# Where the values of an attention unit stand in the DMA queue of a hybrid decoder block

## The chip, the cores and the metric

The kernel runs on one core of a Trainium2 chip. The metric is the device time of one execution in microseconds (us); shorter is better. The core has TensorE (PE, matrix products), VectorE (DVE), ScalarE (ACT), GpSimd (POOL) and SyncE (SP); SP issues all the data transfers (DMAs) of this kernel, in one queue and in a fixed order, and 16 DMA engines carry them out. Each engine works through its own list of instructions in order and waits, where it has to, for a semaphore that another engine or a DMA raises. TensorE writes to PSUM, the other tiles lie in SBUF, and DRAM tiles hold what is put aside.

## The reference

A decoder block for x of 1024 positions by 1024 channels, in float32: a normalisation, one wide projection, two attention branches side by side, gates, an output projection and a normalisation again. Cut to the two branches:

```python
qa, ka, va, fa, za, qb, kb, vb, zb, gates = jnp.split(rms_norm(x, g_pre) @ w_in, ...)
# branch a: 8 heads of 64, with a forget gate; c = cumsum(log_sigmoid(fa + b_forget))
p = softmax(causal(qa @ ka.T / 8 + c[t] - c[s]));    ya = (p @ va) * silu(za)
# branch b: 4 heads of two query/key pairs of 64 (rotated by rope), values of 128
p = softmax(causal(q1 @ k1.T / 8)) - lam * softmax(causal(q2 @ k2.T / 8))
yb = rms_norm(p @ vb, g_subln) * (1 - lam_init) * silu(zb)
merged = sigmoid(gate_a) * (ya @ w_branch[0]) + sigmoid(gate_b) * (yb @ w_branch[1])
out = x + rms_norm(merged @ w_out, g_post)
```

## The kernel before, in words

Products are made in two parts: each float32 operand is split into a rounded high part and the rest (`hi`, `lo`), and three products (hi by hi, hi by lo, lo by hi) are summed in PSUM.

**Stage 1** (lines 119 to 222) normalises and transposes x into `hT`, projects the values of all heads (`v_block`, tiles `pv`) and puts them aside in DRAM as `vb_d` (branch b) and `va_d` (branch a), split into both parts. It ends at about 110 us of the span.

**Stage 2** (lines 251 to 647) is the attention. It has eight units: units 0 to 3 are the four heads of branch b ("diff", tile names that end in d), units 4 to 7 two heads each of branch a ("fox", names in f). For a unit u:

- `unit_proj` (line 271) projects keys and queries, in two chunks of 512 positions each, with weights loaded and split by `load_w` (line 225: `raw_k`, `raw_q`, `hi_k`, `lo_k` and so on). For diff units `rope` (line 280) copies the PSUM tile to `rawk` or `rawq` (line 283), swaps its quarters by four DMAs into `swk` or `swq` (line 287), multiplies `raw` by the cosines on VectorE (line 288) and `sw` by the sines on GpSimd (line 289), and adds them (line 290). `stack` (line 293) then writes the high and low parts into `TA`, `TB` (queries) and `KA`, `KB` (keys).
- `swapped` (line 401) makes the exchanged queries `X0` and `X1` of a group of 256 positions: two DMAs each (line 407), which swap the upper and lower halves of `TA` or `TB`. There are three buffers of each, so they can be made ahead.
- `s_row` (line 410) computes the scores of 128 positions in PSUM (lines 421 and 422; the second takes X), VectorE takes them over with the mask and their row minimum (line 423), ScalarE takes the exponential (line 428), VectorE the reciprocal (line 430).
- `av` (line 433) transposes the probabilities (line 450), splits them (lines 453, 454) and multiplies them by the values `V` (line 474); `evac` writes the result to DRAM (`y_d`, lines 523 and 555).
- `unit_attn` (line 485) allocates the value tile `V` of the unit (line 489: 128 partitions by 8 by 256 values, two buffers) and gives back `load` and the list of `groups`. `load` issues the DMA of `V` (line 495) and, for fox units, two broadcasts `cb` (line 500).

The loop over units (lines 618 to 645) calls `unit_attn(u, T)` and `load()` first. Then it goes through the groups: 4 in a diff unit, 8 in a fox unit (4 per head). It traces the rows of a group, then the `av` of the group before it (`pend`), then a share of `fill`: the projections of the next unit, those of the gate paths `z` (tiles `pz`), and small work. So the last `av` of unit u comes behind the first rows of unit u+1.

**What sets the order.** The tracing order is not the order of execution. When the program is built, a planner with a timeline of its own (`schedule_with_timeline_sim=True`, line 1011) places each instruction on its engine's list as soon as its inputs are there and its buffer is free by that timeline; what was traced earlier goes first among those that are ready. `V` has two buffers, so both unit 0's and unit 1's are free from the start, and V of unit u has to wait for the last product of unit u-2.

**Stages 3 and 4** (lines 654 to 972) compute the gates, the branch products and the output projection. The change does not touch them.

Of the kernel before, what the change touches and what calls it, by code (L numbers as in the profile page):

```python
# [41 lines left out]
def f32(ap):  # L42
    return ap.bitcast(F32)
# [3 lines left out]
def tile_hybrid_block(  # L47
# [18 lines left out]
    nc = tc.nc  # L66
# [184 lines left out]
    with ExitStack() as st:  # L251
# [75 lines left out]
        def z_tasks(t):  # L327
            return spill_tasks(f"z{t}", (ZA + t * P) if t < 4 else (ZB + (t - 4) * P), z_d[t])
# [72 lines left out]
        def swapped(T, m, g, nm):  # L401

            src = T["TB" if m else "TA"]
            qs = slice(2 * g * P, (2 * g + 2) * P)
            t = qk.tile([P, 2 * P], F32R, tag=f"X{m}", name=f"X{m}{nm}_{g}", bufs=3)
            for a, b in ((UPR, DNR), (DNR, UPR)):
                nc.sync.dma_start(f32(t[a]), f32(src[b, qs]))
            return t

        def s_row(T, m, i, X, bias, boff, nm):  # L410

            A, B = (T["TA"], T["KA"]) if m == 0 else (T["TB"], T["KB"])
            n = (i + 1) * P
            qs = slice(i * P, (i + 1) * P)
            xs = slice(i % 2 * P, (i % 2 + 1) * P)
            pr = pp.tile([P, S], F32, tag="P", name=f"P{nm}_{m}_{i}")
            mx = small.tile([P, 2], F32, tag="mx", name=f"mx{nm}_{m}_{i}", bufs=8)
            pcs = pieces(i)
            for j, (a, b) in enumerate(pcs):
                ps = sps.tile([P, CH], F32, tag="S", name=f"S{nm}_{m}_{i}_{j}")[:, 0:b - a]  # L420
                nc.tensor.matmul(ps, lhsT=A[:, qs], rhs=B[:, a:b], start=True, stop=False)  # L421
                nc.tensor.matmul(ps, lhsT=X[:, xs], rhs=B[:, a:b], start=False, stop=True)
                nc.vector.tensor_tensor_reduce(  # L423
                    out=pr[:, a:b], in0=ps, in1=bias[:, boff + a:boff + b], scale=-0.125,
                    scalar=BIG if j == 0 else mx[:, j - 1:j], op0=ALU.add, op1=ALU.min,
                    accum_out=mx[:, j:j + 1])
            le = small.tile([P, 1], F32, tag="l", name=f"l{nm}_{m}_{i}", bufs=8)
            nc.scalar.activation(pr[:, 0:n], pr[:, 0:n], AF.Exp,  # L428
                                 bias=mx[:, len(pcs) - 1:len(pcs)], scale=-1.0, accum_out=le)
            nc.vector.reciprocal(le, le)  # L430
            return pr, le
# [53 lines left out]
        def unit_attn(u, T):  # L485

            diff = u < 4
            t = u if diff else u - 4
            vt = qk.tile([P, NB, 256], F32R, tag="V", name=f"V{u}")
            src = (vb_d if diff else va_d)[:, t, :].rearrange("(b p) c -> p b c", p=P)  # L490
            cb = []
            groups = []

            def load():
                nc.sync.dma_start(f32(vt), src)
                if not diff:
                    for m in range(2):
                        b = big.tile([P, S], F32, tag="big", name=f"cb{u}_{m}")
                        h = 2 * t + m
                        nc.sync.dma_start(b, cum_d[h:h + 1, :].to_broadcast([P, S]))  # L500
                        cb.append(b)

            if diff:
                def row(i, rows):
                    boff = S - (i + 1) * P
                    if "X" not in rows:
                        rows["X"] = [swapped(T, m, i // 2, f"d{u}") for m in range(2)]
                    p1, l1 = s_row(T, 0, i, rows["X"][0], dmask, boff, f"d{u}")
                    p2, l2 = s_row(T, 1, i, rows["X"][1], dmask, boff, f"d{u}")
                    n = (i + 1) * P  # L510
                    nc.vector.tensor_tensor(l2, l2, nlam, op=ALU.mult)  # L511
                    nc.gpsimd.tensor_scalar(  # L512
                        p2[:, 0:n], p2[:, 0:n], l2, 1.0, op0=ALU.mult, op1=ALU.mult)
                    nc.scalar.activation(p1[:, 0:n], p1[:, 0:n], AF.Copy, scale=l1)
                    nc.gpsimd.tensor_tensor(
                        p1[:, 0:n], p1[:, 0:n], p2[:, 0:n], op=ALU.add)
                    rows[i] = p1

                def evac(g):
                    def run(yp):  # L520
                        ys = stg.tile([P, 2 * P], F32, tag="ys", name=f"ys{u}_{g}")
                        nc.scalar.copy(ys, yp)
                        nc.sync.dma_start(y_d[u][:, g * 2 * P:(g + 1) * 2 * P], ys)
                    return run

                for g in GORD[u]:
                    rows = {}
                    groups.append((
                        4 * g + 3,
                        [lambda i=i, rows=rows: row(i, rows) for i in (2 * g, 2 * g + 1)],  # L530
                        lambda g=g, rows=rows: av(rows, g, vt, 0, False, evac(g), f"d{u}_{g}", False)))
            else:
                ysb = {}

                def row(m, i, rows):
                    n = (i + 1) * P
                    diag = cb[m][:, n - P:n]
                    nc.gpsimd.tensor_tensor(diag, diag, trim, op=ALU.add)  # L538
                    if "X" not in rows:
                        rows["X"] = swapped(T, m, i // 2, f"f{u}")  # L540
                    p1, l1 = s_row(T, m, i, rows["X"], cb[m], 0, f"f{u}")
                    nc.gpsimd.tensor_scalar(  # L542
                        p1[:, 0:n], p1[:, 0:n], l1, 1.0, op0=ALU.mult, op1=ALU.mult)
                    rows[i] = p1

                def evac(m, g):
                    def run(yp):
                        if m == 0:
                            ysb[g] = stg.tile([P, 2 * P], F32, tag="ys", name=f"ys{u}_{g}")
                        tmp = stg.tile([P, 2 * P], F32, tag="yt", name=f"yt{u}_{m}_{g}", bufs=1)  # L550
                        nc.scalar.copy(tmp[64:128], yp[64:128])
                        nc.vector.tensor_tensor(
                            ysb[g][64 * m:64 * m + 64], yp[0:64], tmp[64:128], op=ALU.add)
                        if m == 1:
                            nc.sync.dma_start(y_d[u][:, g * 2 * P:(g + 1) * 2 * P], ysb[g])
                    return run

                for g in GORD[u]:
                    for m in range(2):
                        rows = {}  # L560
                        groups.append((
                            4 * g + 3,
                            [lambda m=m, i=i, rows=rows: row(m, i, rows) for i in (2 * g + 1, 2 * g)],
                            lambda m=m, g=g, rows=rows: av(
                                rows, g, vt, m * P, True, evac(m, g), f"f{u}_{m}_{g}",
                                u == 7 and g in FING)))
            return load, groups


        lt = pp.tile([P, 4, 64], F32, tag="P", name="lt")  # L570
# [43 lines left out]
        T, tasks = unit_proj(0)  # L614
        for tk in tasks:
            tk()
        pend = None
        for u in range(8):
            load, groups = unit_attn(u, T)
            if u == 1:  # L620
                forget_sums()
            load()
            fill = []
            if u + 1 < 8:
                T, tasks = unit_proj(u + 1)
                fill += tasks
            for t in ZFILL[u]:
                fill += z_tasks(t)
            fill[2:2] = [lambda k=k: h_combinations(k) for k in TFILL[u]]
            for t in SFILL[u]:  # L630
                fill += [lambda t=t, c=c: sum_squares(t, c) for c in range(2)]
                fill.append(lambda t=t: subln_scales(t))
            total = sum(s[0] for s in groups)
            done, nf = 0, 0
            for n, (wgt, rws, prd) in enumerate(groups):
                for r in rws:
                    r()
                if pend:
                    pend()
                pend = prd  # L640
                done += wgt
                while nf < len(fill) and nf < len(fill) * done / total:
                    fill[nf]()
                    nf += 1
# [370 lines left out]
```

## Time and profile before

| what | value |
|---|---|
| median of 3 runs | 958.73 us |
| lowest, highest | 956.02, 959.63 us |
| the profiled execution's own time | 960.13 us |
| its span, first to last instruction | 958.0 us |
| its mean granted TensorE clock | 0.982 |

How to read the lines quoted below. Times are microseconds, unless a mean is marked ns. L495 is line 495 of the kernel. A tile's buffer number and unit are left out of its name: `V<-vb_d` is a load of any diff unit's values, `X0d<-TA` an exchange. In a line in order of time the first number is the start, counted from the start of the span, the second the duration, x2 the number of instructions merged into the line; brackets hold the idle time before it and what ended that. SPq is SP's queue: its durations are those of the issue, not of the transfer. In a view by stretches the columns are the stretch, its length, busy time of PE, PEld (weight loads, which overlap with PE), DVE, ACT and POOL, each with its count, then the granted TensorE clock as a share of full speed, the mean busy share of the 16 DMA engines, and GB/s.

### The profile page before, as it was taken

The numbers are of one execution on the slowest core, as the hardware profiler recorded it, in microseconds if no ns is written. First come the engines' busy times: TensorE is split into PE (matmuls) and PEld (weight loads), VectorE is DVE, ScalarE is ACT, GpSimd is POOL, SyncE is SP. The second block draws the span as 40 slices with busy tenths as digits, with TensorE's granted clock in tenths as the row PEclk, the third lists the DMA queues.
The fourth block names the chain that finished last, engine by engine and source line by source line (L and its number), as shares of the span: only waits on it lengthen the run. The fifth ranks groups of instructions, "written<-read, shape, count | busy, mean of one in ns | idle before, by whom it ended". The sixth has DMA issues, their size and how long they took to land.

```text
span 958.0 us, 13760 instructions
## 1 busy us (share of the span) xinstructions
PE 900.7 (94%) x4600; PEld 752.1 (79%) x4600; DVE 627.2 (65%) x1180; ACT 437.0 (46%) x862; POOL 489.6 (51%) x460
## 2 busy tenths in 40 slices
PE   7999989899999999999999988999999999999992
PEld 5999867787887888888878877777888768887871
DVE  7731258978768868578676478228665782559875
ACT  3521125665656574565745658323443550324331
POOL 7200035446545466464644575216655735878972
PEclk9999999999999999999999999998999989999997
DMA  9532454434334353534434350893445696210144
GB/s 314 193 110 91 142 134 114 105 80 123 97 94 138 95 155 116 154 122 130 143 123 136 103 186 28 325 377 122 139 138 172 186 370 203 73 38 1 48 150 154
DMA packets 115656, 136.95 MB, mean 143 GB/s; under 512 B 10609, under 2 KB 80241, under 8 KB 114562
## 3 DMA queue, kind: packets, MB, share of 16 engines
q1 hardware_dynamic: 115586, 136.08, 44.4%
q8 instruction: 36, 0.59, 0.3%
q14 instruction: 34, 0.28, 0.1%
HBM read 85.65 MB, written 37.81 MB: 129 GB/s over the span
## 4 chain that ended last, share of the span: by engine, by line
PE 58%; DVE 13%; POOL 8%; DMA 7%; issue 6%; ACT 5%; SPq 2%; DVEq 0%; POOLq 0%; ACTq 0%
PE x_g L713 11%; PE pv L195 9%; PE pb L848 9%; PE pz L246 7%; PE pk L246 4%; PE pq L246 3%; PE ypf L474 3%; PE pg L246 2%; PE ptf L450 2%; DMA swk<-rawk 2%; SPq L287 1%; DVE Pd L423 1%; PE ypd L474 1%; PE Sf L421 1%; DVE wo_op L890 1%
## 5 line engine op out<-in xcount | busy, mean ns | idle before, releaser
L195 PE MATMUL pv<-wvhi,hT 128*128 128x264 f32 (+2 forms) x384 | 89.3, 325 | 0.4 <-DVE hT L181 0.4
L246 PE MATMUL pk<-hT,hi_k 128*128 128x512 f32 x256 | 83.9, 401 | 4.2 <-DVE KB L298 2.4
L246 PE MATMUL pz<-hT,hi_z 128*128 128x512 f32 x256 | 85.1, 400 | 0.0
L848 PE MATMUL pb<-yT,hi_br 128*128 128x512 f32 x256 | 80.8, 398 | 1.9 <-ACT hi_br L232 1.6
L246 PE MATMUL pq<-hT,hi_q 128*128 128x512 f32 x256 | 82.3, 395 | 0.0
L713 PE MATMUL x_g<-T,a_g 128*128 128x512 f32 x336 | 79.5, 392 | 1.6 <-ACT a_g L664 1.2
L713 PE MATMUL x_o<-wo_op,a_o 128*128 128x512 f32 x336 | 77.4, 391 | 2.4 <-ACT a_o L664 1.2
L713 PEld LDWEIGHTS x_o<-wo_op,a_o 128*128 128x128 f32 x336 | 62.8, 188 | 16.9 <-ACT a_o L664 2.1
L713 PEld LDWEIGHTS x_g<-T,a_g 128*128 128x128 f32 x336 | 63.5, 190 | 15.7 <-ACT a_g L664 1.6
L195 PEld LDWEIGHTS pv<-wvhi,hT 128*128 128x128 f32 x384 | 64.6, 190 | 6.2 <-DVE hT L181 0.7
L542 POOL TENSOR_SCALAR Pf<-Pf,lf 128x1024 f32<-128x1024 f32 (+3 forms) x64 | 52.5, 824 | 30.2 <-DVE lf L430 27.4
L713 PE MATMUL x_g<-hT,a_g 128*128 128x512 f32 x252 | 62.0, 400 | 2.6 <-ACT a_g L664 2.0
L428 ACT ACTIVATE Pf<-Pf,mxf 128x1024 f32<-128x1024 f32 (+3 forms) x64 | 49.8, 778 | 32.1 <-DVE mxf L423 29.5
L428 ACT ACTIVATE Pd<-Pd,mxd 128x128 f32<-128x128 f32 (+7 forms) x64 | 49.5, 774 | 30.0 <-DVE mxd L423 28.2
L538 POOL TENSOR_TENSOR cb<-cb,trim 128x128 f32<-128x128 f32 x64 | 30.0, 470 | 62.9 <-DVE mxf L423 45.1
L195 PE MATMUL pv<-wvlo,hT 128*128 128x512 f32 (+2 forms) x192 | 61.9, 325 | 0.0
L512 POOL TENSOR_SCALAR Pd<-Pd,ld 128x128 f32<-128x128 f32 (+7 forms) x32 | 25.6, 799 | 68.8 <-DVE ld L511 38.2
L848 PEld LDWEIGHTS pb<-yT,hi_br 128*128 128x128 f32 x256 | 49.1, 193 | 13.1 <-ACT hi_br L232 2.0
L713 PEld LDWEIGHTS x_g<-hT,a_g 128*128 128x128 f32 x252 | 48.5, 193 | 13.7 <-ACT a_g L664 2.4
L246 PEld LDWEIGHTS pk<-hT,hi_k 128*128 128x128 f32 x256 | 47.6, 190 | 14.4 <-DVE KB L298 2.5
L454 DVE TENSOR_TENSOR plf<-ptf,phf 128x512 fp32r<-128x512 f32 (+1 forms) x80 | 49.6, 633 | 10.1 <-ACT phf L453 9.5
L246 PEld LDWEIGHTS pz<-hT,hi_z 128*128 128x128 f32 x256 | 47.9, 191 | 8.7
(243 smaller groups left out, 2426.6 us busy)
## 6 DMA issues: line engine op xcount, KB each, us to landing
t_d<-t SPq DMA_DIRECT2D x32, 256.0 KB, 2.2
T<-t_d SPq DMA_DIRECT2D x8, 1024.0 KB, 14.9
raw<-in_w_in_dram SPq DMA_DIRECT2D x14, 512.0 KB, 4.1
g_d<-c_g SPq DMA_DIRECT2D x21, 256.0 KB, 3.9
vb_d<-vbs SPq DMA_DIRECT2D x8, 512.0 KB
va_d<-vas SPq DMA_DIRECT2D x8, 512.0 KB, 3.8
raw_k<-in_w_in_dram SPq DMA_DIRECT2D x8, 512.0 KB, 5.3
raw_q<-in_w_in_dram SPq DMA_DIRECT2D x8, 512.0 KB
```

The source lines that it names most:

```text
L195: nc.tensor.matmul(ps[n], lhsT=hT[hp][k // 4][i // 4][:, k % 4, hs], rhs=wt[k][:, a:b], start=first, stop=(k == KT - 1 and hp == 1))
L246: nc.tensor.matmul(ps, lhsT=a[:, k, :], rhs=hT[h][k // 4][c][:, k % 4, :], start=(k == 0 and a is hi and h == 0), stop=(k == KT - 1 and a ...
L287: nc.sync.dma_start(sw[b * 32:(b + 1) * 32, :], raw[o * 32:(o + 1) * 32, :])
L428: nc.scalar.activation(pr[:, 0:n], pr[:, 0:n], AF.Exp, bias=mx[:, len(pcs) - 1:len(pcs)], scale=-1.0, accum_out=le)
L450: nc.tensor.transpose(pt[:, o * P:(o + 1) * P], rows[2 * g + r][:, j * P:(j + 1) * P], ident)
L454: nc.vector.tensor_tensor(pl[:, 0:n], pt[:, 0:n], ph[:, 0:n], op=ALU.subtract)
L474: nc.tensor.matmul(o, lhsT=a, rhs=b[:, src], start=(j == 0 and n == 0), stop=(odd == 1 and jj == g and n == len(prods) - 1))
L512: nc.gpsimd.tensor_scalar(p2[:, 0:n], p2[:, 0:n], l2, 1.0, op0=ALU.mult, op1=ALU.mult)
L538: nc.gpsimd.tensor_tensor(diag, diag, trim, op=ALU.add)
L542: nc.gpsimd.tensor_scalar(p1[:, 0:n], p1[:, 0:n], l1, 1.0, op0=ALU.mult, op1=ALU.mult)
L713: nc.tensor.matmul(x[m], lhsT=a[:, ai, k, :], rhs=right[m][bi][k], start=(k == 0 and n == 0), stop=(k == 3 and n == 2))
L848: nc.tensor.matmul(ps, lhsT=a[:, kk, :], rhs=yT[g][h][:, k % 2, sl], start=(k == 0 and a is hi and h == 0), stop=(k == 3 and a is lo))
```

## The change

The load of `V` is taken out of `load` and becomes `load_v`, which is not called at the start of the unit. It is put into a list, `vload`, and `swapped`, whenever it finds something there, calls it once behind its own two DMAs. `tc.issue_after` adds an edge that orders the load behind the second of these on SP's list, without a semaphore.

- Unit 0's load is put in the list ahead of its first group, so it goes behind the X0 of unit 0's group 0.
- For the others, `unit_attn(u + 1, T)` is now called ahead of the middle group of unit u (the third of 4, or the fifth of 8), which allocates the tile there, and the load goes behind the first exchange of that group. The result is kept in `nxt` and used when the loop comes to unit u+1.

The broadcasts `cb` stay in `load`. No transfer is added or left out, and none changes in size.

```diff
             for a, b in ((UPR, DNR), (DNR, UPR)):
-                nc.sync.dma_start(f32(t[a]), f32(src[b, qs]))
+                lastx[0] = nc.sync.dma_start(f32(t[a]), f32(src[b, qs])).ins
+            if vload:
+                with tc.issue_after(lastx[0]):
+                    vload.pop(0)()
             return t
+
+        lastx, vload = [None], []
...
+            def load_v():
+                nc.sync.dma_start(f32(vt), src)
+
             def load():
-                nc.sync.dma_start(f32(vt), src)
                 if not diff:
...
-            return load, groups
+            return load, load_v, groups
...
         pend = None
+        nxt = None
         for u in range(8):
-            load, groups = unit_attn(u, T)
+            load, load_v, groups = nxt or unit_attn(u, T)
+            nxt = None
+            if u == 0:
+                vload.append(load_v)
...
             for n, (wgt, rws, prd) in enumerate(groups):
+                if n == len(groups) // 2 and u < 7:
+                    nxt = unit_attn(u + 1, T)
+                    vload.append(nxt[1])
                 for r in rws:
```

## The prediction

> **What bounds the kernel now.** I read the page first, then busy time by stretch, then the waits and the order of time of each engine in the one stretch that stands out, and last every place where values (V) and exchanged queries (X) are issued.
>
> ```profile
> span 958.0 us, 13760 instructions
> ...
> PE 900.7 (94%) x4600; PEld 752.1 (79%) x4600; DVE 627.2 (65%) x1180; ACT 437.0 (46%) x862; POOL 489.6 (51%) x460
> ```
>
> TensorE (PE) is the bound as a whole. The change touches only the attention stage, 113 to 603 us. The columns below are the length of the stretch, then the busy time of PE, of its weight loads, of VectorE (DVE), ScalarE (ACT) and GpSimd (POOL), then the granted clock.
>
> ```profile
> 113.00:180.00 67.00, 58.48 (x265) 46.77 (x264) 47.91 (x90) 27.12 (x58) 25.53 (x22) 0.97 0.48 129
> 180.00:603.00 423.00, 408.11 (x2278) 344.70 (x2277) 310.59 (x776) 259.56 (x544) 226.28 (x244) 1.00 0.39 117
> ```
>
> PE idles 8.5 us in the first 67 us, and 14.9 us in the next 423. From 180 us on PE has nearly no holes, so whatever the start of the stage gives PE is carried to the end, and little more can be found later. Where do the 8.5 us lie? Three rows hold 7.8 of them: two of PE in order of time, with the wait in brackets,
>
> ```profile
> 134.99 0.70 PE L246 MATMUL pk<-hT,hi_k 128*128 128x512 f32 x2 [1.73 <-ACT rawk L283]
> 137.74 0.50 PE L246 MATMUL pk<-hT,lo_k 128*128 128x512 f32 x1 [2.04 <-DVE lo_k L236]
> ```
>
> and one of PE's waits in this stretch (total, times, longest):
>
> ```profile
> PE Sd L421 <- DVE mxd L423: 4.0, 3, 1.9
> ```
>
> The two waits around 135 us have one origin. DVE sat idle until the swapped keys (swk) of unit 0 had landed,
>
> ```profile
> 129.31 0.69 DVE L288 TENSOR_TENSOR rawk<-rawk,cosT 128x512 f32<-128x512 f32 x1 [8.70 <-DMA swk<-rawk]
> ```
>
> and the chain of waits runs through just that transfer (start, length):
>
> ```profile
> 123.64 5.54 DMA swk<-rawk
> ```
>
> And this is what stands ahead of swk in SP's queue (start, issue time):
>
> ```profile
> 113.88 1.41 SPq L495 DMA_DIRECT2D V<-vb_d  x2
> 117.07 2.39 SPq L228 DMA_DIRECT2D raw_q<-in_w_in_dram  x1
> 119.56 4.68 SPq L287 DMA_DIRECT2D swk<-rawk  x4
> 124.33 4.34 SPq L287 DMA_DIRECT2D swq<-rawq  x4
> 134.87 2.41 SPq L287 DMA_DIRECT2D swk<-rawk  x4
> 138.43 1.15 SPq L407 DMA_DIRECT2D X0d<-TA  x2
> 139.67 1.19 SPq L407 DMA_DIRECT2D X1d<-TB  x2
> 140.96 2.44 SPq L287 DMA_DIRECT2D swq<-rawq  x4
> ```
>
> The values of units 0 and 1 are both fetched at 113.9 us, and yet nobody reads any of them before this:
>
> ```profile
> 162.46 0.40 PE L474 MATMUL ypd<-phd,V 128*128 128x256 f32 x2
> ```
>
> **The change part by part.**
>
> *V0 and V1 leave the head of the queue.* Sizes of one issue, and the median landing in us:
>
> ```profile
> V<-vb_d SPq DMA_DIRECT2D x4, 1024.0 KB
> swk<-rawk SPq DMA_DIRECT2D x32, 64.0 KB, 2.0
> ```
>
> What the DMA engines did meanwhile (last columns: clock, busy share, GB/s):
>
> ```profile
> 120.00:122.00 2.00, 2.00 (x11) 1.65 (x10) 0.31 (x2) 0.20 (x1) 0.00 (x0) 1.00 1.09 354
> 122.00:124.00 2.00, 2.00 (x10) 1.69 (x9) 0.00 (x0) 0.59 (x1) 0.00 (x0) 1.00 1.11 339
> ```
>
> The engines are saturated. One V is 1.05 MB, at some 345 GB/s 3.0 us; two are 6.1 us. A second reckoning uses swk's own rows: its four issues took 4.68 us where the later set took 2.41 (2.27 too long), and it landed 5.54 us after the chain left its issue, where 2.0 is the median (3.54 too long): 5.8 us. If the issue of raw_q, 2.39 us, was held too, at most 2.0 more: 7.8. So swk lands 5.8 to 7.8 us earlier than 129.2; I take 6.8, near the middle and a little above the bytes' 6.1: 122.4.
>
> *What is late next.* Queries need the same swap. ScalarE copies them out, and DVE takes them up:
>
> ```profile
> 122.42 0.59 ACT L283 COPY rawq<-pq 128x512 f32<-128x512 f32 x1 [2.19 <-PE pq L246]
> ```
>
> ```profile
> 132.87 1.52 DVE L288 TENSOR_TENSOR rawq<-rawq,cosT 128x512 f32<-128x512 f32 x1
> 136.47 1.22 DVE L236 TENSOR_TENSOR lo_k<-raw_k,hi_k 128x1024 fp32r<-128x1024 f32 x1
> ```
>
> PE's own pace sets rawq, ready at 123.0. Four issues of 2.4 us in all and 2.0 us to land bring swq to 127.4, and the product by the cosines, which overwrites rawq, cannot start before. It starts 5.4 us earlier than 132.87. So 5.4 of the 6.8 us reach the DVE chain, and the rest becomes a wait for swq.
>
> *What PE gets.* PE runs out of work at 134.99 - 1.73 = 133.3. With DVE 5.4 us ahead, lo_k is ready at 137.7 - 5.4 = 132.3, and the copy of rawk that frees the PSUM buffer stands behind casts that move as much. Both waits go: 1.73 + 2.04 = 3.8 us. The clock also fell right behind this hole:
>
> ```profile
> 138.00:140.00 2.00, 2.00 (x6) 1.56 (x6) 1.94 (x3) 0.45 (x1) 1.09 (x1) 0.55 0.23 58
> 140.00:142.00 2.00, 2.00 (x8) 1.57 (x7) 1.90 (x2) 0.00 (x0) 1.72 (x2) 0.60 0.40 99
> ```
>
> At 0.55 and 0.60 granted, 0.9 + 0.8 = 1.7 us of PE work are lost; without the hole they should not be. PE's side of the gain is 5.5 us.
>
> *V0 in its new place.* It now stands between X0d and X1d of group 0, and chunk 1's swq stands behind both. GpSimd shows when that swq came before:
>
> ```profile
> 145.01 1.30 POOL L289 TENSOR_TENSOR swq<-swq,sinT 128x512 f32<-128x512 f32 x1 [3.29 <-DMA swq<-rawq]
> ```
>
> Moved up by 5.4, X0d is issued from 133.0 to 134.2, V0 until 134.7, X1d until 135.9, swq until 138.4. V0's bytes begin about 2 us behind its issue, at 136.2, and take 3.0; the 0.38 MB behind it take 1.1 more: swq lands at about 140.6, still 4.4 us before 145.0. V0 thus eats between nothing and 1.0 of DVE's 5.4. X1d is under the same delay and also stays ahead of its old time. V0 itself lands near 139.5; its first reader, moved up by 5, stands at 157.5.
>
> *V1 in its new place* goes between X0d and X1d of unit 0's group 2. X1d's issue there, and PE's first use of it:
>
> ```profile
> 152.57 1.19 SPq L407 DMA_DIRECT2D X1d<-TB  x2
> ```
>
> ```profile
> 160.71 0.34 PE L422 MATMUL Sd<-KB,X1d 128*128 128x384 f32 x1
> ```
>
> Issued by 153.8, landed by 155.8 at 2.0, read at 160.7: 4.9 us of cover for 3.0 us of V1. Cost nothing. Without that cover it is 3.0 us at most.
>
> *V2 to V7* get the same edge, but their buffer is free long after it. Unit 1's group 2 is exchanged at 187, and V2 is issued only when unit 0's last product has let its buffer go:
>
> ```profile
> 187.07 1.11 SPq L407 DMA_DIRECT2D X0d<-TA  x2
> ...
> 226.73 0.53 SPq L495 DMA_DIRECT2D V<-vb_d  x1
> ```
>
> The edge is met already, so these six move only as far as their earlier place in the program changes the planner's choice: nothing in the sum. No instruction is added or removed anywhere, and the edge adds no wait to any engine but the order on SP.
>
> *A rule against the change.* The Trainium skill, "DMA: Bandwidth & Descriptors", section "Rules for kernel authors", advises to overlap a DMA with compute by issuing it early and waiting for it late; by that rule the old place is the better one. The trace shows early issue buying nothing for V0, 48 us ahead of its reader, and charging swk 5.8 us or more; by the row the gain stands, by the rule alone it would be a loss.
>
> **Sum.** PE's side gives 5.5 us, DVE's 5.4 less 0 to 1.0 for V0, hence 4.4 to 5.5. I take 5.0. The 4.0 us in which PE waits for DVE's row minima stay, since DVE and PE move up by about the same. The profiled execution took 960.13 us with its span of 958.0, 1.4 us above the median of 958.73. The sum is a difference in one stage, so I take it off the median: 953.7. If all 6.8 us came through it would be 951.9.
>
> **The rivals.**
>
> *Given back within the stretch.* DVE is busy nearly all the time from 130 to 180 us; the V transfers, 3.0 us each, now stand amid swaps and exchanges of that very chain. If V0 costs all its 3.0 us and V1 a further 1, 5.0 becomes 1.0: 957.7. For it: the chain there is made of short transfers that are awaited at once. Against: the margins above, 4.4 and 4.9 us.
>
> *More than forecast.* If the planner, with swk on time, also fills the 4.0 us of waits for row minima, the hole shrinks by 5.0 + 4.0: 949.7. For it: DVE would get lo_z and lo_k of later weights done earlier. Against: the same DVE work remains.
>
> *Slower: V at the head of the queue.* V2 to V7 are now traced half a unit earlier, and so go ahead of more in SP's queue. There a V holds everything behind it until its buffer is free. That happened before, by the longest row of SP's waits; the X behind it, and its first use, follow.
>
> ```profile
> SPq L495 <- PE ypf L474: 4.5, 1, 4.5
> ```
>
> ```profile
> 452.04 1.36 SPq L407 DMA_DIRECT2D X0f<-TA  x2
> ```
>
> ```profile
> 462.87 0.47 PE L422 MATMUL Sf<-KA,X0f 128*128 128x512 f32 x1
> ```
>
> The X behind V6 is read 10.8 us after its issue began. A hold of 4.5 us and 3.0 us of transfer fit in that. Beyond a hold of 7.8 us each further one reaches PE. A hold of 10 us costs 2.2 us in each of five units (V3 to V7), 11 us; less 5.0, that is 6 slower: 964.7. It decides from a hold of some 8.8 us, where the five units eat the gain. Against it: PE waits for no X anywhere, and the planner has to misjudge the buffer by twice what it did before.
>
> *Late values.* V0 comes after its reader. It would have to land over 18 us later than reckoned (157.5 less 139.5), because the queue put something long ahead of X0d; each further microsecond is PE's. At 23 us late it undoes the gain, at 28 it costs 10 less 5.0: 963.7. This is the direction in which the rule above points.
>
> *The edge does nothing* for six of eight loads already in the forecast; if V0 and V1 were not what held swk (the DMA rates say they were), the time would stay at 958.7.
>
> **How the numbers follow.** A measurement of this kernel can tell about 0.5% from no change, 4.8 us. The forecast, 951.9 to 955.5, has a chance of 0.58, of which 0.40 lie beyond 4.8 us, since 5.0 is only just over it, and 0.18 within. More than forecast: 0.08. Given back, or nothing: 0.19, all within 0.5%. V at the head of the queue: 0.12; late values: 0.03; both slower. Faster 0.48, same 0.37, slower 0.15. The likeliest case's own range stands above; for 8 in 10 the range reaches down to 949.0, about the case of more, and up to 961.0, past the given-back case into the first part of the slower ones.
>
> **What would show it.** Right: no V in SP's queue ahead of raw_q and swk; swk landed near 122 to 123 us, DVE's idle time before the first rotation down from 8.7 to about 2; no PE wait on lo_k or rawk at 133 to 138 us and full clock there; V0 issued right behind the first X0d and landed well ahead of the first product with V; V2 to V7 still issued when their buffer comes free; everything from 180 us on 5 us earlier. Wrong: DVE waiting for X1d's scores or for swq right behind V0, V1 in front of a swap that PE then waits for, SP held at V for over 8 us, or PE's idle time from 180 to 603 us grown beyond 14.9.

## The result, and the profile after

The changed kernel takes 951.7 us (median of 6 runs, 949.8 to 954.59) against 958.12 us before (6 runs, 956.02 to 959.63). The ratio is 0.9935 with a 95% interval of 0.9912 to 0.9958, that is 6.2 us or 0.65% faster. A second measurement, told below, gave 0.9943 (0.9919 to 0.9966). The forecast was 953.7, or 5.0 us faster, with 951.9 to 955.5 for the likeliest case: the median lies 0.2 us under the lower end of that, inside the wider range of 949.0 to 961.0.

The profiled execution took 953.12 us with a span of 951.1, against 958.0. Where did 6.9 us go? First SP's queue of the changed kernel in order of time, at the place where the two V stood before:

```profile
117.70 0.38 SPq L228 DMA_DIRECT2D raw_q<-in_w_in_dram  x1
118.18 2.51 SPq L287 DMA_DIRECT2D swk<-rawk  x4
123.67 2.41 SPq L287 DMA_DIRECT2D swq<-rawq  x4
129.10 2.41 SPq L287 DMA_DIRECT2D swk<-rawk  x4
135.70 1.15 SPq L407 DMA_DIRECT2D X0d<-TA  x2
136.90 0.58 SPq L500 DMA_DIRECT2D V<-vb_d  x1
137.57 1.21 SPq L407 DMA_DIRECT2D X1d<-TB  x2
138.88 2.46 SPq L287 DMA_DIRECT2D swq<-rawq  x4
```

No V stands ahead of raw_q and swk any more, the issues take 0.38 and 2.51 us instead of 2.39 and 4.68, and V0 stands right behind the first X0d. Next VectorE (DVE), in order of time, with the idle time before each row in brackets:

```profile
123.21 0.69 DVE L288 TENSOR_TENSOR rawk<-rawk,cosT 128x512 f32<-128x512 f32 x1 [4.50 <-DMA swk<-rawk]
...
129.44 0.69 DVE L288 TENSOR_TENSOR rawq<-rawq,cosT 128x512 f32<-128x512 f32 x1 [1.57 <-DMA swq<-rawq]
...
144.68 0.69 DVE L288 TENSOR_TENSOR rawq<-rawq,cosT 128x512 f32<-128x512 f32 x1 [3.13 <-DMA swq<-rawq]
```

The first rotation starts at 123.21 instead of 129.31. This execution reached the end of the value projection 0.6 us later than the other (its last product starts at 110.9 instead of 110.3), so it is 6.7 us earlier in the kernel. But the last row shows that most of this lead is gone by the second chunk's queries: 144.68 against 145.08 before.

To see what PE has of it, I cut the attention of each kernel into three stretches: 35 us from its own last product of the value projection, the next 35 us, and the rest up to its first product of the gates. The columns used are the stretch, its length, PE's busy time, and, third from the end, the granted clock. Length less busy time is PE's idle time; busy time by what the clock lacks to 1.00 is the loss to the clock. Before:

```profile
110.30:145.30 35.00, 30.62 (x130) 24.32 (x129) 17.35 (x26) 6.74 (x13) 7.61 (x6) 0.95 0.48 136
145.30:180.30 35.00, 30.86 (x151) 24.88 (x150) 31.35 (x67) 20.90 (x47) 17.92 (x17) 0.98 0.46 115
180.30:603.20 422.90, 407.81 (x2278) 344.50 (x2276) 310.47 (x776) 259.42 (x543) 226.48 (x244) 1.00 0.39 117
```

and after:

```profile
110.90:145.90 35.00, 32.88 (x148) 26.44 (x147) 17.02 (x27) 7.57 (x16) 9.10 (x6) 1.00 0.40 113
145.90:180.90 35.00, 31.65 (x152) 24.54 (x151) 30.76 (x68) 20.41 (x43) 19.68 (x17) 1.00 0.62 162
180.90:598.80 417.90, 401.88 (x2259) 341.71 (x2257) 310.56 (x773) 260.00 (x545) 227.41 (x244) 1.00 0.39 117
```

In the first stretch PE lost 4.4 us to idleness and 1.5 to the clock; now it is 2.1 and 0: 3.8 us gained. In the second, 4.1 and 0.6 became 3.4 and 0: 1.3 gained. In the rest idleness went from 15.1 to 16.0; the clock cost some 1.1 us there before and 1.6 after, summed over windows of 4 us (the 1.00 of the whole stretch is too coarse for it). The attention as a whole went from 492.9 to 487.9 us: the 5.0 us of the forecast. Idleness and clock explain 3.7 of them (3.8 + 1.3 - 0.9 - 0.5); what the other 1.3 are, the profile does not say. Of the remaining difference of the spans, 0.6 us was lost ahead of the attention and 2.5 gained behind it, in code that the change doesn't touch. That part moves from one execution to the next: in the branch products (line 848, 862 after) the longest of 256 took 794 ns before and 500 after, but 792 again in the second profile of the changed kernel. It goes with the clock: from 760 to 780 us 0.83 was granted before, 1.00 after, and 0.83 in that second profile.

PE's row with the longest wait for a transfer in that first stretch, and the first reader of V0:

```profile
143.85 0.30 PE L427 MATMUL Sd<-KB,X1d 128*128 128x128 f32 x1 [0.91 <-DMA X1d<-TB]
...
160.72 0.40 PE L479 MATMUL ypd<-phd,V 128*128 128x256 f32 x2
```

The other six loads stayed where their buffer lets them be. V2's issue, the exchange that the edge puts it behind, and SP's longest wait at such a load:

```profile
188.03 1.17 SPq L407 DMA_DIRECT2D X0d<-TA  x2
...
224.28 0.56 SPq L500 DMA_DIRECT2D V<-vb_d  x1
```

```profile
SPq L500 <- PE ypf L479: 4.5, 1, 4.5
```

### The profile page after: what moved, and what is told of

Same layout as the page of the kernel before. It is cut to its first block, busy times and chain, and to the rows that moved or that the text cites. A ratio compares the mean times of both kernels' runs of the same rounds, so it can differ in the third digit from the quotient of the medians.

```text
span 951.1 us, 13757 instructions
## 1 busy us (share of the span) xinstructions
PE 894.2 (94%) x4600; PEld 748.2 (79%) x4600; DVE 624.7 (66%) x1180; ACT 437.4 (46%) x862; POOL 493.5 (52%) x460
## 4 chain that ended last, share of the span: by engine, by line
PE 52%; DVE 14%; POOL 12%; DMA 8%; issue 7%; ACT 5%; SPq 2%; DVEq 0%; POOLq 0%; ACTq 0%
PE pb L862 9%; PE pv L195 9%; PE pz L246 7%; PE pk L246 4%; PE pq L246 4%; PE x_g L727 4%; PE ypf L479 3%; PE pg L246 2%; PE ptf L455 2%; POOL S_g L691 2%; DMA raw<-in_w_in_dram 2%; DMA swq<-rawq 2%; PE Sf L426 1%; DVE Pd L428 1%; PE Sf L427 1%
## 5 line engine op out<-in xcount | busy, mean ns | idle before, releaser
L246 PE MATMUL pk<-hT,hi_k 128*128 128x512 f32 x256 | 81.1, 394 | 2.0 <-DVE KB L298 1.9
L679 DVE TENSOR_TENSOR a_g<-S_g,a_g 128x512 fp32r<-128x512 f32 x28 | 30.8, 1102 | 36.6 <-ACT a_g L678 36.6
```

Of the source, the lines that this page charges most:

```text
L246: nc.tensor.matmul(ps, lhsT=a[:, k, :], rhs=hT[h][k // 4][c][:, k % 4, :], start=(k == 0 and a is hi and h == 0), stop=(k == KT - 1 and a ...
L679: eng.tensor_tensor(lo, src, hi, op=ALU.subtract)
```

## The experiments

The theory was: two loads at the head of the queue hold the first swap, and PE runs dry; taking them out gives 5 us, and V2 to V7 do nothing. The main rival after the result: each edit makes the planner order the rest of the attention anew, and the gain is a matter of that order. Every kernel was measured beside the kernel before on the same chip. "Lost" is idleness and clock together, reckoned as above from each kernel's own profile. The conditions in the code cuts are written shorter than in the kernels.

| kernel | ratio to before (95%) | lost in first 35 us | in next 35 us | idle in the rest | attention, us |
|---|---|---|---|---|---|
| before | 1 | 5.9 | 4.8 | 15.1 | 492.9 |
| changed | 0.9935 (0.9912 to 0.9958) | 2.1 | 3.4 | 16.0 | 487.9 |
| changed, again | 0.9943 (0.9919 to 0.9966) | 2.3 | 3.4 | 14.6 | 487.2 |
| only V0, V1 moved | 0.9958 (0.9937 to 0.9980) | 2.6 | 3.4 | 18.2 | 490.9 |
| only V2 to V7 moved | 1.0000 (0.9979 to 1.0020) | 5.9 | 4.0 | 16.5 | 494.8 |
| only V1 moved | 0.9928 (0.9902 to 0.9954) | 1.4 | 5.4 | 13.3 | 486.2 |
| V0, V1 not loaded | 0.9957 (0.9937 to 0.9977) | 0.7 | 6.5 | 14.6 | 490.2 |
| V0 behind X1d, group 0 | 0.9920 (0.9893 to 0.9947) | 0.6 | 2.8 | 14.4 | 483.8 |
| V0 behind X1d, group 1 | 0.9925 (0.9897 to 0.9952) | 0.7 | 5.2 | 15.1 | 486.7 |
| and V1 behind X1d, group 3 | 0.9978 (0.9962 to 0.9994) | 0.9 | 8.5 | 14.9 | 492.1 |
| three MB at the head | 0.9988 (0.9973 to 1.0004) | 8.7 | 2.3 | 15.0 | 491.7 |
| V2 to V7 behind the second group | 0.9918 (0.9890 to 0.9946) | 0.6 | 3.1 | 14.2 | 483.2 |
| V2 to V7 behind the last group | 0.9963 (0.9945 to 0.9982) | 0.6 | 3.1 | 17.5 | 488.0 |
| V0 behind X1d, V2 to V7 not moved | 0.9927 (0.9904 to 0.9950) | 1.1 | 4.4 | 13.2 | 486.4 |

Three cautions for this table. Its last three columns come from one execution each: that of "V2 to V7 behind the second group" took 946.68 us, the shortest of six that go up to 954.57. And the clock is left out of "idle in the rest"; by windows of 4 us it cost there from nothing (three MB) to 4.7 us ("and V1 behind X1d"). And a loss reckoned from a whole stretch's clock can be off by some 0.3 us: with three MB the first stretch's 2.9 are 2.6 by windows of 1 us.

**Only V0 and V1 moved.** V2 to V7 are loaded at the start of their unit again:

```diff
-                if n == len(groups) // 2 and u < 7:
+                if n == len(groups) // 2 and u + 1 in (0, 1):
...
+            if u not in (0, 1):
+                load_v()
             load()
```

> Only V0 and V1 go behind the exchanges; V2 to V7 are loaded at the start of their unit as before. Theory (what counts is that the two loads leave the head of SP's queue): as the full change, 5 to 7 us under before, with SP's list up to 170 us that of the changed kernel. Rival (the gain comes from the earlier place of V2 to V7 in the planner's order): 0 to 2 us under before.

It is 4.0 us faster by the ratio (1.9 to 6.0), between what the two expected. Its stretches:

```profile
111.40:146.40 35.00, 32.42 (x145) 25.97 (x144) 17.09 (x27) 7.14 (x14) 8.78 (x6) 1.00 0.40 111
146.40:181.40 35.00, 31.59 (x149) 24.44 (x148) 29.76 (x67) 20.06 (x43) 20.07 (x17) 1.00 0.64 164
181.40:602.30 420.90, 402.69 (x2263) 341.40 (x2262) 313.46 (x774) 261.12 (x546) 227.81 (x244) 1.00 0.39 116
```

The first two are those of the changed kernel, 2.6 and 3.4 us lost; in the third PE idles 18.2 us, 2.2 more than there. So the start comes from V0 and V1 alone, and part of it is lost again much later.

**Only V2 to V7 moved.** The counterpart:

```diff
-            if u == 0:
-                vload.append(load_v)
+            if u < 2:
+                load_v()
             load()
...
-                if n == len(groups) // 2 and u < 7:
+                if n == len(groups) // 2 and 0 < u < 7:
```

> Only V2 to V7 get the new place; V0 and V1 stay at the head of the queue. Theory: within 2 us of before, swk of unit 0 still landing near 129 us, each V still issued when its buffer comes free. Rival: 4 to 6 us under before.

Ratio 1.0000. The first stretch is the one of before, with the same loss of 4.4 + 1.5 us:

```profile
110.80:145.80 35.00, 30.64 (x130) 24.43 (x129) 17.35 (x26) 6.72 (x13) 7.60 (x6) 0.95 0.48 137
```

The rival that the earlier place of V2 to V7 brings the gain falls.

**Only V1 moved,** V0 stays at the head:

```diff
-            if u == 0:
-                vload.append(load_v)
+            if u != 1:
+                load_v()
             load()
...
-                if n == len(groups) // 2 and u < 7:
+                if n == len(groups) // 2 and u + 1 == 1:
```

> Only V1 leaves the head; V0 stays there, V2 to V7 stay. One megabyte instead of two ahead of swk. Theory: swk lands about 3 us earlier than before, at 126 us, PE's hole at 133 to 138 us shrinks by about 3 us, and the time is 2 to 4 us under before; not much less than the full change if V0 in its new place costs DVE the 3 us that the wait for swq at 144.7 us shows. Rival (a threshold: any load at the head is as bad as two): within 1 us of before.

It was faster than expected: 6.9 us by the ratio (4.4 to 9.4), as good as the full change. DVE's first rotation, and the first two stretches:

```profile
127.08 0.69 DVE L288 TENSOR_TENSOR rawk<-rawk,cosT 128x512 f32<-128x512 f32 x1 [5.24 <-DMA swk<-rawk]
```

```profile
111.30:146.30 35.00, 33.61 (x152) 27.16 (x151) 19.68 (x35) 8.66 (x20) 9.20 (x6) 1.00 0.44 118
146.30:181.30 35.00, 31.21 (x145) 24.73 (x144) 31.73 (x67) 20.41 (x42) 19.63 (x18) 0.95 0.57 152
```

This execution reached the attention 1.0 us later than before, so the swap is 3.2 us earlier: one megabyte, as reckoned. Idleness shrank by 3.0 us, from 4.4 to 1.4, and in this stretch the loss to the clock is gone altogether. So one of the two loads could have stayed at the head for 0.8 us of PE's time in the first stretch (1.4 lost here against 0.6 at the best). But the clock falls in the next stretch instead, at 168 us, and costs some 1.6 of its 5.4 us.

How the clock's loss comes can be seen in windows of 1 us. Before, from 138 to 142 us, 0.60, 0.50, 0.50 and 0.69 are granted: together 1.7 us lost, as much as 3.4 us at one half. In this kernel, from 168 to 173, it is 0.93, 0.50, 0.50, 0.50 and 0.86, 1.7 us again. So it comes in a whole piece or not at all. Which wait brings one, its length doesn't tell. PE's rows with the last wait ahead of a piece, in the kernel before and in this one, and then one with a longer wait (the kernel with V0 behind X1d of group 1), after which 1.00 goes on being granted:

```profile
177.97 0.44 PE L421 MATMUL Sd<-KA,TA 128*128 128x384 f32 x1 [1.87 <-DVE mxd L423]
...
167.42 0.39 PE L426 MATMUL Sd<-KA,TA 128*128 128x256 f32 x1 [2.10 <-DVE mxd L428]
...
198.94 0.60 PE L616 MATMUL ft<-ident,fs 128*8 128x128 f32 x4 [2.79 <-DVE fs L607]
```

The Trainium skill, "TensorE: Matmul & The Clock Gate", section "Part 1: The HAM clock gate (the "warmup" mystery)", says that the clock drops to one half after an idle window of some 3.4 us. The half agrees with the 0.50 granted here; the idle time does not, since no wait quoted here is that long and two of some 2 us brought a fall where one of 2.79 brought none.

**V0 and V1 not loaded.** Meant as the bound:

```diff
             def load_v():
-                nc.sync.dma_start(f32(vt), src)
+                if u < 2:
+                    nc.gpsimd.memset(f32(vt), 0.5)
+                else:
+                    nc.sync.dma_start(f32(vt), src)
```

and `load_v()` is called at the start of each unit again.

> The values of units 0 and 1 are not loaded at all: GpSimd fills the two tiles with a constant while it idles at 110 to 120 us, so two products work on constants; V2 to V7 stay as before. The bound on what any place for the two loads can give. Theory, with V0 and V1 costing about 3 us in the changed kernel's places (3.1 us of DVE's wait for swq, 0.9 us of PE's for X1d): 7 to 10 us under before. If those places cost nothing on the path: 5 to 7, as the changed kernel. Rival (the head of the queue was not the cause): within 2 us of before.

```profile
111.20:146.20 35.00, 34.28 (x156) 28.04 (x155) 19.48 (x37) 10.51 (x23) 13.95 (x10) 1.00 0.37 95
146.20:181.20 35.00, 30.05 (x139) 23.46 (x138) 31.44 (x67) 18.52 (x40) 18.78 (x16) 0.95 0.46 115
```

The first stretch is as the theory wants it, 0.7 us lost: 5.2 less than before. But the time is only 4.1 us under before (2.2 to 6.0). In the next stretch PE loses 6.5 us, 1.7 more than before; 1.5 of the 6.5 are the clock, behind a wait of 1.88 us for DVE's row minima. A kernel with less to do is no faster than the changed one: so this is no bound, and what lies behind the first stretch is not simply moved up with it.

**The changed kernel again, and V0 in three other places.** Four kernels on one chip. In the last three `vload` counts the calls of `swapped`:

```diff
-            if vload:
+            ncall[0] += 1
+            if vload and ncall[0] > vload[0][0]:
                 with tc.issue_after(lastx[0]):
-                    vload.pop(0)()
+                    vload.pop(0)[1]()
...
-                vload.append(load_v)
+                vload.append((1, load_v))
```

with 1 for "behind X1d of group 0", 3 for "behind X1d of group 1". V1's entry has 4, which leaves it behind X0d of group 2, and 7 for "behind X1d of group 3".

> The changed kernel once more, beside the next three on one chip: 5 to 7.5 us under before.

> V0 behind X1d of group 0 instead of X0d; the planner puts it behind chunk 1's swq as well. The rest is as in the changed kernel. Theory (V0 between X0d and X1d costs the chain about 3 us): swq lands near 141 instead of 144.7, no PE wait for X1d, and the time is 1 to 3 us under the changed kernel. Rival (V0's place is hidden by other work): within 1 us of the changed kernel.

> V0 behind X1d of group 1, the rest as in the changed kernel. Theory: as with V0 behind X1d of group 0, 1 to 3 us under the changed kernel; V0 lands near 147, ahead of its first reader at about 155. Rival 1 (hidden anyway): within 1 us of the changed kernel. Rival 2 (now it stands ahead of the next unit's weights and swap, which PE then waits for): 1 to 3 us above the changed kernel.

> V0 behind X1d of group 1 and V1 behind X1d of group 3 of unit 0. Theory, with V1's old margin of 4.9 us for 3.0 us of transfer: the same as with V0 alone moved there, within 1 us. Rival (V1 between X0d and X1d of group 2 costs the chain too): 1 to 3 us less again.

With V0 behind X1d of group 0, the second chunk's queries and the stretches are:

```profile
139.77 0.69 DVE L288 TENSOR_TENSOR rawq<-rawq,cosT 128x512 f32<-128x512 f32 x1
```

```profile
111.20:146.20 35.00, 34.44 (x157) 28.34 (x156) 21.61 (x41) 11.24 (x25) 10.41 (x8) 1.00 0.49 131
146.20:181.20 35.00, 32.23 (x151) 24.92 (x151) 27.75 (x62) 19.08 (x38) 20.08 (x16) 1.00 0.55 139
```

swq is taken up 4.9 us earlier than in the changed kernel, and PE loses 0.6 us where that lost 2.1 to 2.3. But this is not V0's place alone, for the first chunk's queries had landed sooner too, before V0 was issued. GpSimd takes them up in the changed kernel and in this one:

```profile
129.47 1.80 POOL L289 TENSOR_TENSOR swq<-swq,sinT 128x512 f32<-128x512 f32 x1 [4.42 <-DMA swq<-rawq]
...
127.94 1.29 POOL L289 TENSOR_TENSOR swq<-swq,sinT 128x512 f32<-128x512 f32 x1 [2.75 <-DMA swq<-rawq]
```

Their last issue ended at 126.08 and 126.34, so they took 3.4 and 1.6 us to land. The records of the DMA packets show why. In the changed kernel a packet of 16 KB on the instruction queue ran from 126.81 to 128.28; all of swq's packets had ended by 127.18 but three, which ended at 128.50 to 128.73. In this kernel swq's packets had ended by 127.44, and the instruction packet ran from 127.40. The eleven profiles without two V at the head all fit this: in eight, the first of the last three packets of swq ends 0.1 to 0.2 us behind the instruction packet, and in three the instruction packet begins only as swq's end. That it holds the three back is inferred from these times; the records do not name the DMA engine.

V0's place can thus only be judged between kernels whose first swq landed alike. Two with a late landing differ by V0's place alone: 2.6 us are lost with it between X0d and X1d (only V0 and V1 moved), 1.1 with it behind X1d (V2 to V7 not moved, below). Where swq landed early, 0.6 are lost with V0 in either place. So V0's first place cost PE some 1.5 us, and only behind a late swq. In time this kernel is 7.7 us under before (5.1 to 10.2), with V0 behind group 1 7.2 (4.6 to 9.9); the changed kernel measured beside them 5.5 (3.3 to 7.8). The intervals overlap: that either beats the changed kernel is likely by the traces and not shown by the times.

With V1 moved too, 0.9978 belies both expectations: the first stretch is as good, 0.9 us, and the second loses 3.9 us to idleness and 4.7 to a clock of 0.85, which stays at 0.50 from 161 to 170 us. PE's longest wait ahead of that, 2.38 us, is for DVE's low parts of the probabilities, not for V. Whether V1's place did that or the order that came with it, these runs don't tell.

**Three megabytes at the head.** The kernel before, with a copy behind V0:

```diff
-                nc.sync.dma_start(f32(vt), src)
+                ld = nc.sync.dma_start(f32(vt), src).ins
+                if u == 0:
+                    with tc.issue_after(ld):
+                        nc.sync.dma_start(spare, vb_d[:, 0, :])
```

> The kernel before with a third megabyte at the head of the queue: behind V0 the same values are also copied to a spare DRAM tile. Theory (bytes ahead of swk set the hole): DVE's first rotation starts about 3 us later than before, near 132 us, PE's loss to idleness and low clock in the 35 us behind the value projection grows from 6.1 to about 9 us, and the time is 2 to 5 us above before. Rival (a threshold that two loads have already passed): within 1 us of before.

```profile
133.85 0.69 DVE L289 TENSOR_TENSOR rawk<-rawk,cosT 128x512 f32<-128x512 f32 x1 [12.19 <-DMA swk<-rawk]
```

```profile
111.00:146.00 35.00, 29.25 (x117) 23.04 (x116) 14.33 (x20) 5.39 (x10) 7.76 (x5) 0.90 0.58 173
146.00:181.00 35.00, 32.73 (x156) 26.44 (x155) 31.16 (x62) 18.46 (x41) 18.74 (x15) 1.00 0.43 106
```

The hole did as the theory said: the first rotation 3.8 us later in the kernel, and 5.8 + 2.9 = 8.7 us lost, 2.8 more. The time did not: 1.1 us under before (2.6 under to 0.4 above). The next stretch loses 2.3 us instead of 4.8 and gives back 2.5 (1.9 of idleness, 0.6 of clock). So the theory fell in one point: what happens in the hole is not by itself the kernel's time.

**V2 to V7 at other places that their buffers can't use.** The changed kernel with one number changed:

```diff
-                if n == len(groups) // 2 and u < 7:
+                if n == (len(groups) // 2 if u == 0 else 1) and u < 7:
```

and, in the other, `len(groups) - 1` in place of 1.

> The changed kernel, but V2 to V7 are put behind the second group's exchange of the unit before instead of the middle one's. Their buffers are not free at either place, so nothing should move on the chip but what the planner orders otherwise. Theory (these six are inert): within 1 us of the changed kernel, 5 to 7 us under before. Rival (what lies behind 180 us is scattered by the planner with every edit): 2 us or more away from the changed kernel, all of it behind 180 us.

> As the last, with V2 to V7 behind the exchange of the unit's last group. Theory: within 1 us of the changed kernel. Rival: 2 us or more away from it, the start up to 180 us being the same.

The second group's place first, then the last group's:

```profile
110.50:145.50 35.00, 34.43 (x157) 28.32 (x156) 19.50 (x30) 9.26 (x18) 9.21 (x6) 1.00 0.47 131
145.50:180.50 35.00, 31.86 (x155) 25.46 (x154) 31.41 (x73) 21.50 (x46) 20.37 (x18) 1.00 0.54 143
180.50:593.70 413.20, 399.03 (x2246) 339.26 (x2244) 308.14 (x766) 257.04 (x539) 225.71 (x243) 1.00 0.39 118
```

```profile
111.60:146.60 35.00, 34.42 (x157) 28.30 (x156) 19.43 (x32) 9.26 (x18) 9.21 (x6) 1.00 0.49 132
146.60:181.60 35.00, 31.91 (x155) 25.54 (x154) 31.59 (x73) 21.50 (x46) 20.38 (x17) 1.00 0.54 143
181.60:599.60 418.00, 400.50 (x2246) 338.75 (x2244) 310.08 (x766) 257.75 (x539) 227.31 (x243) 1.00 0.39 117
```

Start and second stretch are the same in both, 0.6 and 3.1 us lost. Yet the rest idles 14.2 us in one and 17.5 in the other, and the ratios are 0.9918 (0.9890 to 0.9946) and 0.9963 (0.9945 to 0.9982): about 4 us apart, with intervals that just touch.

What the two edits did to the order can be read from the traces, instruction by instruction on PE, DVE, ACT, POOL and SP. The second group's kernel has the changed kernel's order throughout: it is a third measurement of it. The last group's kernel has throughout the order of "only V0, V1 moved", which leaves the changed kernel's at some 277 us. So there are three measurements of one order, 0.9918 to 0.9943 with 14.2 to 16.0 us idle in the rest, and two of the other, 0.9958 and 0.9963 with 18.2 and 17.5. The theory holds for the second group's place, where nothing moved, and the rival for the last group's: the place of these six loads is worth some 2.5 us there by the order alone, an estimate that the intervals leave uncertain by about 2. One and the same order differs by up to 2.4 us from one measurement to another.

The start shows that scatter too. V0 stands between X0d and X1d here as in the changed kernel, in the same order, but the first swq landed early (DVE takes it up at 127.27 instead of 129.44), X0d is issued 3.3 us sooner (0.4 of it this execution's own lead), and V0's place costs almost nothing:

```profile
132.39 1.15 SPq L407 DMA_DIRECT2D X0d<-TA  x2
133.59 0.58 SPq L500 DMA_DIRECT2D V<-vb_d  x1
```

**V0 behind X1d, V2 to V7 not moved.** The first of the three other places of V0, and from unit 2 on the loads of before:

```diff
-                if n == len(groups) // 2 and u < 7:
+                if n == len(groups) // 2 and u == 0:
...
+            if u > 1:
+                load_v()
             load()
```

> V0 behind X1d of group 0 and V1 as in the changed kernel, V2 to V7 at their unit's start as before. Theory: the first 70 us behind the value projection lose 3.4 us of PE as with V0 behind X1d and all eight moved, and the time is 6 to 8 us under before. If V2 to V7 in their earlier place were worth 2 us, as the difference of the two kernels that share the changed kernel's start suggests: 4 to 6 us under before.

7.0 us under before (4.8 to 9.2), as the theory had it in time, but not in the stretches: 1.1 and 4.4 us lost, and 13.2 idle in the rest, the least of all. That V2 to V7 in their earlier place are worth 2 us, as the first kernel suggested, is not borne out here: without them the rest idles 13.2 us, with them (V0 behind X1d, group 0) 14.4. Those two kernels have one order up to some 274 us, and yet lose 4.4 and 2.8 us in the second stretch.

## Why the prediction was right, and where it was not

**Direction, size and chief cause: right.** 5.0 us were forecast for the attention, and the profiled attention is 5.0 us shorter; that the two agree so closely is luck, by the errors told below. The first 35 us lose 5.9 us wherever two V stand at the head of the queue and 0.6 to 2.6 where V1 is gone from it, in ten kernels with eight different orders. That the head of the queue makes the hole is shown, from three megabytes down to none.

**swk's time: right.** 122.4 was reckoned; 123.21, less the 0.6 us by which this execution was late, is 122.6. DVE's idle time ahead of it was to fall to about 2 us and fell to 4.5, because the small lambda loads also came sooner and DVE began to wait earlier.

**swq next, 5.4 us earlier than 132.87: a little too much.** It began at 129.44, 4.0 us earlier in the kernel; the landing took 3.4 us behind the last issue where the sum had the median's 2.0. In the three kernels where no instruction packet came in between it took 1.6, so the chain was right and this term was too short by a delay that the prediction did not have.

**PE's hole: right.** Both waits at 133 to 138 us and the low clock are gone. Idleness and clock fell by 3.8 us in place of 5.5.

**V0 in its new place, "between nothing and 1.0": the term that was mis-sized.** It used X0d at 133.0, by moving the old time up by 5.4. X0d was issued at 135.70, 2.7 us later: 2.0 because the first queries' product began at 129.44 in place of 127.5 (0.6 of that is this execution's own delay), and 0.7 net because DVE then waited 1.18 us for GpSimd's product and took 1.52 and 1.67 us for the sum and for TA, 0.69 each before. V0 and the two transfers behind it came so much later, and swq was taken up at 144.68 in place of 140.6. Of DVE's lead 1.0 us was left there, and PE paid some 1.5 us. This is nearly all that the hole's 3.8 lacks to 5.5. With swq on time, V0 in this place cost nothing that shows.

**"The 4.0 us in which PE waits for DVE's row minima stay": wrong by 1.3 us.** The second stretch lost 3.4 us instead of 4.8, and these waits fell from 4.0 to 2.8. The two errors cancel in the sum. The other kernels show that this stretch goes from 2.3 to 8.5 us, and from 2.8 to 4.4 with one and the same order, so here the forecast was lucky.

**V2 to V7, "nothing in the sum": right for the queue, too simple for the time.** Each was issued when its buffer came free, and SP waited 4.5 us at the most, as before, so V at the head of the queue did not come about. But their earlier place gave another order behind 277 us, worth some 2.5 us to the changed kernel; with V0 behind X1d the rest was no better for it.

**The rule against the change,** to issue a DMA early (the Trainium skill, "DMA: Bandwidth & Descriptors", section "Rules for kernel authors"), is bounded by these runs: one V issued early cost 0.8 us of PE's time in the first stretch, two cost 5.3 (5.9 against 0.6), and V0 at its new place was still in time for its reader.

**What stays open.** Why the second stretch gives back 2.5 us where the hole was larger, and takes 1.7 where no V was loaded. The clock is 0.6 and 0.9 of that; that the planner's order of DVE's work does the rest is argued, not shown. When a wait makes the clock fall, and what sets the time of the instruction packet that delays swq, is open too.

## What to carry to other kernels

A transfer that nobody needs for 48 us is not free if it stands ahead of a short one that the next engine awaits: look at what follows it in the queue, and move it until the hole closes, which need not mean moving all of it. Look also at what it then stands ahead of, as X1d and swq here. Where a planner orders the engines anew at each edit, compare the orders in the traces before you explain a difference: two kernels here were repeats of others. What repeats of one order differ by, up to 2.4 us here, is the least that a gain must exceed before a time alone can prove it.

## What the runs showed of the hardware

The clock's loss comes in pieces: one half is granted for some 3.4 us, or two or three times as long, 1.7 us of PE's work each. Single waits of 1.87 and 2.10 us were followed by a piece and one of 2.79 us was not. A short transfer can land late without any load of the kernel in front of it: swq took 3.4 us in place of 1.6 where a 16 KB packet on the instruction queue ran before its last packets. An issue also takes longer behind a full queue: with two megabytes just queued ahead of it in the three-megabyte kernel, that of V1 took 4.30 us on SP, where V0's had taken 0.38.
